# Mixer A: turning the attention probabilities with VectorE block transposes and placing copies instead of TensorE, with two query groups in flight

## The chip, the cores and the metric

The kernel runs on one core of one Trainium2 chip. The metric is the device time of one execution, in microseconds. The profiler gives the span of one execution beside it, with every instruction of TensorE (PE; weight loads: PEld), VectorE (DVE), ScalarE (ACT), GpSimd (POOL) and the DMA queue of SyncE (SP).

## The reference

The model is an encoder trunk of two layers on 256 tokens of 2048 features, in float32. Each layer is a token mixer and a gated MLP with a depthwise convolution, both behind an RMSNorm and with a residual add. The first layer uses mixer A, the second mixer B (three dilated head groups). The change is in mixer A: 16 query heads in 4 groups, each group with one key and one value head of 128 features; keys and queries are normalised per head and rotated.

```
def attend(q_blk):
    logits = jnp.einsum('bqkgd,bskd->bkgqs', q_blk, k).astype(jnp.float32) * scale
    p = jax.nn.softmax(logits, axis=-1).astype(v.dtype)
    return jnp.einsum('bkgqs,bskd->bqkgd', p, v)
```

Scores come out with queries on the partitions and keys along the free axis, which suits the softmax. The product with v sums over keys, so the probabilities have to be turned first: keys on the partitions. For one head that is a 256x256 transpose, held as two query halves m of 128 partitions by 256 keys.

## The kernel before

The tokens are split over 128 partitions and two halves m. Every float32 matmul is done as three products of rounded parts: an operand is split into a high part (ScalarE copy to fp32r) and a low part (VectorE subtraction), and TensorE adds high x high, high x low and low x high (L153 to L155 in `feed`, L307 to L309 in `mm3`). Weights come as 512 KB blocks through SP's queue (L145) into six raw tiles and are split by `split_raw` (L128 on ScalarE, L129 on VectorE) into a ring of three pairs wh, wl.

A projection (`project`) makes four calls of `feed` for one 512-wide output block. Each call issues two halves of 12 matmuls, and after each half it calls `step()`, so that a projection has eight steps. Work between projections is written as Python generators. `start` runs one to its first yield and puts it in the list `pending`; `step` advances the first of the list by one yield. If the list `wide` is not empty, `step` advances the first two instead. `drain` steps until the list is empty.

Mixer A first projects keys and values, then calls for the four query groups `start(attend(g, project(...)))`, then the output projection `out_proj`. So the attention of group g runs between the matmuls of projection g+1, and that of group 3 beside the first part of the output projection. `project2` in `out_proj` runs three quarters of two output blocks, drains, and then takes the last quarter, which reads the heads of group 3.

`attend(g)` begins with `qk_post`: ScalarE evacuates and squares, VectorE and GpSimd multiply with the rotary tables (L799, L804, L806), GpSimd raises to the power -0.5 (L390, its result rqk). Two steps later TensorE transposes the queries (`heads_T`, L703). Then come six stages, one step each: in stage k the scores, maxima and exps of head k (L846 to L860), the transposes of the probabilities of head k-1 (L868: four 128x128 TensorE transposes into a PSUM tile, then the split into pTh and pTl, L871), and the product with v for head k-2 with the split into its slot pair ah, al (L879 to L883). Nine steps in all, so a group's last stage falls on the first step of the next projection but one.

A second way of transposing exists already, `turned`, used for keys, for the residual and in mixer B: VectorE transposes all 32x32 blocks of a 128x512 half in one instruction each (L335), and `place_blocks` copies 16 sets of 32 partitions to where they belong. A string of four letters says which engine places which block: p is GpSimd, a ScalarE, v VectorE.

The order on each engine is not the order of the program. The framework has a planner that puts an instruction that is ready, by its own estimate of times, ahead of one that isn't, and otherwise goes by priority, which is program order. `split_raw` is given a priority 45 instructions earlier (AHEAD). Once planned, each engine runs its queue in order. The framework also sets the waits between engines by what is read and written of each tile, and gives a tile's place to its successor only when all its readers are done.

Slots: the pairs ah0 to ah23 and al0 to al23 hold the heads' outputs in mixer A (0 to 15) and mixer B (0 to 23), the activations in the MLP, and some probabilities in mixer B.

Of the kernel before, what the change touches and what calls it, by code (L numbers as in the profile page):

```python
# [7 lines left out]
F32 = mybir.dt.float32  # L8
# [25 lines left out]
def tile_encoder(ctx: ExitStack, tc: tile.TileContext, x, xT, w_a, w_ao, q_gain, k_gain, w_b, w_bo,  # L34
# [25 lines left out]
    def nm(s):  # L60
        uid[0] += 1
        return f"{s}_{uid[0]}"
# [353 lines left out]
    def ffn(l, hT, ss_in, g_next, last, side=None):  # L416
        with tc.tile_pool(name=nm("wpool"), bufs=1) as wp, tc.tile_pool(name=nm("fpool"), bufs=1) as fp:
# [101 lines left out]
            for hf, (p0, p1) in enumerate(HALVES):  # L519
# [197 lines left out]
    def mixer_a():  # L717
        with tc.tile_pool(name="apool", bufs=1) as ap:
# [110 lines left out]
            def attend(g, accs):  # L829
# [9 lines left out]
                prs, pTs, ots = {}, {}, {}  # L839
                for k in range(6):  # L840
                    yield
                    if k < 4:
                        i = k
                        s = ps_tile()
                        for m in range(2):
                            mm3(s[:, m * NT:(m + 1) * NT], qT, kT,  # L846
                                (slice(None), i, slice(m * P, (m + 1) * P)), (slice(None), g), True, True)
                        mx = small.tile([P, 2], F32, tag="mx", name=nm("mx"), bufs=3)
                        nc.vector.tensor_reduce(mx, s.rearrange("p (m c) -> p m c", m=2), axis=AX.X,
                                                op=ALU.max, negate=True)  # L850
                        nc.vector.tensor_tensor(mx, mx, rqv[:, :, i], ALU.mult)
                        pr = ap.tile([P, 2, NT], F32, tag="pr", name=nm("pr"), bufs=2)
                        l = small.tile([P, 2], F32, tag="l", name=nm("l"), bufs=3)
                        for m in range(2):
                            nc.scalar.activation(pr[:, m, :], s[:, m * NT:(m + 1) * NT], AF.Exp,
                                                 bias=mx[:, m:m + 1], scale=rq[:, 4 * m + i:4 * m + i + 1],
                                                 accum_out=l[:, m:m + 1])
                        nc.vector.reciprocal(l, l)
                        for m in range(2):
                            nc.vector.tensor_scalar(pr[:, m, :], pr[:, m, :], l[:, m:m + 1], None, op0=ALU.mult)  # L860
                        prs[i] = pr
                    if 1 <= k < 5:
                        i = k - 1
                        pr = prs.pop(i)
                        t = ps_tile()
                        for m in range(2):
                            for kt in range(2):
                                nc.tensor.transpose(t[:, kt * NT + m * P:kt * NT + (m + 1) * P],  # L868
                                                    pr[:, m, kt * P:(kt + 1) * P], ident)
                        pTs[i] = pair_tile(ap, [P, 2 * NT], "pT", 2)  # L870
                        split(pTs[i][0], pTs[i][1], t)  # L871
                    if k >= 2:
                        i = k - 2
                        pT = pTs.pop(i)
                        if i % 2 == 0:
                            ot = ps_tile()
# [261 lines left out]
```

## Time and profile before

| | us |
|---|---|
| median of 3 runs | 2264.49 (2264.11 to 2266.11) |
| profiled execution, its own time | 2266.43 |
| span of the profiled execution | 2264.6 |
| TensorE busy in the span | 2247.2 |
| VectorE busy | 1658.6 |
| ScalarE busy | 1511.0 |
| GpSimd busy | 257.7 |

The chain that ended last goes through TensorE for 80% of the span. Mixer A takes about the first 216 us; the probability transposes (L868) start between 93.7 and 198.5 us. A page row of an instruction group names line, engine, operation, the tiles, the shape and the count, then busy time and mean duration, then the idle time in front and what ended it. A row by source line or tile gives the least, median and longest duration in ns. A timeline row gives start, duration, engine, line and operation, with merged neighbours counted by x.

### The profile page before, as it was taken

What the parts mean: (1) busy time and instruction counts of PE and PEld (TensorE: products, weight loads), DVE (VectorE), ACT (ScalarE), POOL (GpSimd) and SP (SyncE); (2) the same over time, 40 slices, a digit from 0 to 9 for tenths busy, and PEclk for the clock granted to TensorE, in tenths of its full rate; (3) what the DMA queues carried; (4) which work ended last, traced back from release to release, by engine and by line L of the source; (5) the groups of instructions that cost most, each with busy time, mean ns of one, the idle gap of its engine ahead of it and who ended that gap; (6) DMA issues with size and microseconds to landing.
All of it is one profiled execution on the core that took longest, in us unless ns stands there. A gap on an engine that the chain in (4) does not pass through costs nothing.

```text
span 2264.6 us, 28910 instructions
## 1 busy us (share of the span) xinstructions
PE 2247.2 (99%) x10157; PEld 1859.7 (82%) x10157; DVE 1658.6 (73%) x2243; ACT 1511.0 (67%) x2344; POOL 257.7 (11%) x372
## 2 busy tenths in 40 slices
PE   9999999999999999999999999999999999999998
PEld 7788888888888888888888888888888888888886
DVE  6776687888878788856565556465888888688895
ACT  6665776777547777767755775565777754577763
POOL 2210112200001010121100100000101100001101
PEclk9999999999999999999999999999999999999999
DMA  8444557755665655666655564565656656556664
GB/s 299 156 149 150 197 196 224 223 188 190 209 205 187 201 189 188 208 218 203 192 172 178 177 193 160 183 195 187 196 192 194 204 186 212 188 191 193 218 202 135
DMA packets 126450, 437.43 MB, mean 193 GB/s; under 512 B 17264, under 2 KB 18032, under 8 KB 126304
## 3 DMA queue, kind: packets, MB, share of 16 engines
q1 hardware_dynamic: 119744, 425.64, 57.5%
q0 software_dynamic: 6128, 9.38, 1.6%
q8 instruction: 79, 1.29, 0.2%
q14 instruction: 67, 0.55, 0.1%
q10 hardware_dynamic: 432, 0.56, 0.1%
HBM read 429.20 MB, written 6.29 MB: 192 GB/s over the span
## 4 chain that ended last, share of the span: by engine, by line
PE 80%; DVE 1%; DMA 1%; ACT 1%; issue 1%; POOL 0%; POOLq 0%; DVEq 0%; ACTq 0%
PE acc L154 21%; PE acc L155 21%; PE acc L153 21%; PE acc L273 5%; PE acc L275 5%; PE acc L278 5%; DMA scr<-lnt 1%; PE ps L305 1%; DVE wl L129 1%; ACT tM L347 0%; PE ps L1016 0%; DMA raw<-in_w_down_dram 0%; ACT wh L128 0%; PE ps L308 0%; PE ps L309 0%
## 5 line engine op out<-in xcount | busy, mean ns | idle before, releaser
L129 DVE TENSOR_TENSOR wl<-raw,wh 128x1024 fp32r<-128x1024 f32 x828 | 1017.7, 1235 | 452.7 <-ACT wh L128 449.8
L128 ACT ACTIVATE wh<-raw 128x1024 fp32r<-128x1024 f32 x828 | 872.9, 1058 | 538.0 <-PE acc L155 325.8
L153 PE MATMUL acc<-wh,xh 128*128 128x512 f32 x2176 | 852.2, 392 | 0.2 <-ACT wh L164 0.2
L154 PE MATMUL acc<-wl,xh 128*128 128x512 f32 x2176 | 848.3, 390 | 3.1 <-DVE wl L129 2.9
L155 PE MATMUL acc<-wh,xh 128*128 128x512 f32 x2176 | 847.4, 389 | 0.0
L154 PEld LDWEIGHTS acc<-wl,xh 128*128 128x128 f32 x2176 | 408.7, 188 | 89.7 <-DVE wl L129 6.3
L155 PEld LDWEIGHTS acc<-wh,xh 128*128 128x128 f32 x2176 | 408.4, 188 | 84.9
L153 PEld LDWEIGHTS acc<-wh,xh 128*128 128x128 f32 x2176 | 408.9, 188 | 83.7 <-ACT wh L164 0.7
L345 POOL COPY u<-t 32x256 f32<-32x256 f32 x176 | 110.7, 629 | 1040.3 <-DVE t L455 1032.2
L273 PE MATMUL acc<-wh,ah 128*128 128x512 f32 x520 | 202.5, 389 | 1.3 <-DVE h L408 1.3
L275 PE MATMUL acc<-wh,al 128*128 128x512 f32 x520 | 202.3, 389 | 0.0
L154 PE MATMUL acc<-wl,ah 128*128 128x512 f32 x480 | 187.1, 390 | 1.0 <-DVE wl L129 1.0
L153 PE MATMUL acc<-wh,ah 128*128 128x512 f32 x480 | 187.3, 391 | 0.1
L155 PE MATMUL acc<-wh,al 128*128 128x512 f32 x480 | 186.6, 389 | 0.0
L347 ACT ACTIVATE u<-t 32x256 f32<-32x256 f32 x352 | 147.8, 420 | 13.8 <-DVE t L455 5.8
L278 PE MATMUL acc<-wl,ah 128*128 128x512 f32 x520 | 146.1, 389 | 0.0
L273 PEld LDWEIGHTS acc<-wh,ah 128*128 128x128 f32 x520 | 97.6, 188 | 22.2 <-DVE h L408 2.0
L278 PEld LDWEIGHTS acc<-wl,ah 128*128 128x128 f32 x520 | 97.6, 188 | 20.3
L275 PEld LDWEIGHTS acc<-wh,al 128*128 128x128 f32 x520 | 97.6, 188 | 20.2
L154 PEld LDWEIGHTS acc<-wl,ah 128*128 128x128 f32 x480 | 90.1, 188 | 20.1 <-DVE wl L129 1.8
L153 PEld LDWEIGHTS acc<-wh,ah 128*128 128x128 f32 x480 | 90.1, 188 | 19.0 <-DVE cu L628 0.6
L155 PEld LDWEIGHTS acc<-wh,al 128*128 128x128 f32 x480 | 90.1, 188 | 18.5
(180 smaller groups left out, 1666.4 us busy)
## 6 DMA issues: line engine op xcount, KB each, us to landing
raw<-in_w_up_dram SPq DMA_DIRECT2D x352, 512.0 KB, 4.3
raw<-in_w_down_dram SPq DMA_DIRECT2D x176, 512.0 KB, 4.8
raw<-in_w_b_dram SPq DMA_DIRECT2D x144, 512.0 KB, 4.3
raw<-in_w_bo_dram SPq DMA_DIRECT2D x48, 512.0 KB, 4.1
raw<-in_w_a_dram SPq DMA_DIRECT2D x40, 512.0 KB, 4.5
raw<-in_w_ao_dram SPq DMA_DIRECT2D x32, 512.0 KB, 3.8
raw<-in_w_a_dram SPq DMA_DIRECT2D x16, 256.0 KB, 6.5
h<-in_x_dram SPq DMA_DIRECT2D x4, 512.0 KB, 8.2
```

Of the source, the lines that this page charges most:

```text
L128: nc.scalar.activation(wh, r, AF.Copy)
L129: nc.vector.tensor_tensor(wl, r, wh.bitcast(F32), ALU.subtract)
L153: nc.tensor.matmul(accs[m], xh, wh[:, j, :], start=st, stop=False)
L154: nc.tensor.matmul(accs[m], xh, wl[:, j, :], start=False, stop=False)
L155: nc.tensor.matmul(accs[m], xl, wh[:, j, :], start=False, stop=sp)
L273: nc.tensor.matmul(acc[k], xh, wh[:, j, :], start=k in fresh, stop=False)
L275: nc.tensor.matmul(acc[k], xl, wh[:, j, :], start=False, stop=False)
L278: nc.tensor.matmul(acc[k], xh, wl[:, j, :], start=False, stop=last[k] == i and j == 1)
L305: nc.tensor.matmul(o, lh[ls], rh[rs], start=start, stop=stop)
L345: nc.gpsimd.tensor_copy(dst, src)
L347: nc.scalar.activation(dst, src, AF.Copy)
```

## The change

The probabilities of mixer A no longer go through TensorE. Per head, VectorE normalises them as before and then transposes all 32x32 blocks in one instruction. Per pair of heads, `place_blocks` with "papa" places 16 blocks, eight by GpSimd and eight by ScalarE. Then each head is split into pTh and pTl, from SBUF.

The stages become ten, one step each, with score of head 0 first and the value product of head 3 last. `wide` is set while mixer A's query groups run, so that two groups advance in each step; it is cleared when the first output block is done. The turned and the placed probabilities lie in four new tiles quad0 to quad3, which take the room of slots 16 to 23, two slots to a quad. These slots become views of the quads everywhere: in the MLP (`new_form`) and in mixer B (`slots`, and pr of its first and third group).

```diff
-    def new_slot(kt):
-        return (hpool.tile([P, NT], F32R, tag=f"ah{kt}", name=nm("ah")),
-                hpool.tile([P, NT], F32R, tag=f"al{kt}", name=nm("al")))
+    quads = {}
+
+    def new_quad(k):
+        return hpool.tile([P, 4, NT], F32, tag=f"quad{k}", name=nm("quad"))
+
+    def new_slot(kt, pool=hpool, dt=F32R):
+        if pool is not hpool or kt < 16:
+            return tuple(pool.tile([P, NT], dt, tag=f"a{c}{kt}", name=nm("a" + c)) for c in "hl")
+        k, i = divmod(kt - 16, 2)
+        if i == 0:
+            quads[k] = hpool.tile([P, 4, NT], dt, tag=f"quad{k}", name=nm("quad"))
+        return quads[k][:, 2 * i], quads[k][:, 2 * i + 1]
...
-                    return tuple(pool.tile([P, NT], F32R, tag=f"a{c}{k}", name=nm("a" + c)) for c in "hl")
+                    return new_slot(k, pool)
...
         def done(accs, n):
+            wide.clear()
             add_residual(accs, n)
...
-                        t = ps_tile()
-                        for m in range(2):
-                            for kt in range(2):
-                                nc.tensor.transpose(t[:, kt * NT + m * P:kt * NT + (m + 1) * P],
-                                                    pr[:, m, kt * P:(kt + 1) * P], ident)
-                        pTs[i] = pair_tile(ap, [P, 2 * NT], "pT", 2)
-                        split(pTs[i][0], pTs[i][1], t)
...
+                def score(i):
+                    if i % 2 == 0:
+                        parts["t", i // 2] = new_quad(i // 2).rearrange("p (m a) c -> p m (a c)", m=2)
...
+                def turn(i):
+                    pr, l = parts.pop(("pr", i)), parts.pop(("l", i))
+                    for m in range(2):
+                        nc.vector.tensor_scalar(pr[:, m, :], pr[:, m, :], l[:, m:m + 1], None, op0=ALU.mult)
+                    c = i % 2 * NT
+                    nc.vector.transpose(parts["t", i // 2][:, :, c:c + NT], pr)
+
+                def place(u):
+                    o = new_quad(2 + u)
+                    place_blocks(o.rearrange("p j (m t) -> p j m t", m=2), parts.pop(("t", u)), "papa")
+                    for i in range(2):
+                        parts[2 * u + i] = o[:, 2 * i:2 * i + 2].rearrange("p a t -> p (a t)")
+
+                def low(i):
+                    src = parts[i]
+                    parts[i] = pair_tile(ap, [P, 2 * NT], "pT", 2)
+                    split(*parts[i], src)
...
+                for fs in ((score, 0), (score, 1, turn, 0), (score, 2, turn, 1), (score, 3, place, 0, turn, 2),
+                           (turn, 3), (place, 1, low, 0), (low, 1, value, 0), (low, 2, value, 1),
+                           (low, 3, value, 2), (value, 3)):
+                    yield
+                    for f, a in zip(fs[::2], fs[1::2]):
+                        f(a)
+
+            wide.append(1)
             for g in range(4):
                 start(attend(g, project(w_a, g, hT, kgs)))
...
-                            pr = [hpool.tile([P, NT], F32, tag=f"a{c}{sl}", name=nm("pr")) for c in "hl"]
+                            pr = list(new_slot(sl, dt=F32))
...
-                            pt = hpool.tile([P, NT], F32, tag=f"ah{sl}", name=nm("pr"))
+                            pt = new_slot(sl, dt=F32)[0]
```

`score` and `value` hold the score and value code of before.

More of the change, by code (lines that the diff above doesn't have):

```diff
@@ new lines, in low, with value @@
+                def low(i):
+                    src = parts[i]
+                    parts[i] = pair_tile(ap, [P, 2 * NT], "pT", 2)
+                    split(*parts[i], src)
+                def value(i):
+                    pT, j = parts.pop(i), i % 2
+                    if j == 0:
+                        parts["o"] = ps_tile()
+                    ot = parts["o"]
+                    for kt in range(2):
+                        mm3(ot[:, j * NT:(j + 1) * NT], v, pT,
+                            (slice(None), kt, slice(g * P, (g + 1) * P)),
+                            (slice(None), slice(kt * NT, (kt + 1) * NT)), kt == 0, kt == 1)
+                    hi, lo = slots[4 * g + i]
+                    split(hi, lo, ot[:, j * NT:(j + 1) * NT])
```

54 lines of the change are left out of this document (17 added, 37 removed).

## The prediction

> **What bounds the kernel now.** I read the head of the page first: which engine fills the span.
>
> ```profile
> span 2264.6 us, 28910 instructions
> PE 2247.2 (99%) x10157; PEld 1859.7 (82%) x10157; DVE 1658.6 (73%) x2243; ACT 1511.0 (67%) x2344; POOL 257.7 (11%) x372
> ```
>
> TensorE is busy in 99% of the span, 17.4 us are left idle. So work taken off TensorE shortens the span, as long as nothing else makes TensorE wait. The change lies in mixer A alone, so the second view is the busy time by window, with windows cut from one first probability transpose of a query group to that of the next:
>
> ```profile
> core 0: us, PE busy (x) PEld busy (x) DVE busy (x) ACT busy (x) POOL busy (x), PEclk, DMA share, GB/s
> 93.69:124.45 30.76, 30.70 (x169) 26.07 (x169) 24.00 (x44) 19.84 (x39) 5.45 (x5) 1.00 0.42 137
> 124.45:155.21 30.76, 30.71 (x169) 26.07 (x169) 23.98 (x44) 19.83 (x39) 5.44 (x5) 1.00 0.43 138
> 155.21:185.97 30.76, 30.72 (x168) 26.06 (x169) 23.98 (x44) 19.83 (x39) 5.45 (x5) 1.00 0.42 139
> ```
>
> Each group takes 30.76 us, and TensorE is busy in 30.7 of it, at a granted clock of 1.00. VectorE has 6.8 us free per group, ScalarE 10.9, GpSimd 25. DMA has room (0.42). The third view is the waits of VectorE and ScalarE in these three periods (total us, times, longest):
>
> ```profile
> ACT wh L128 <- PE acc L155: 11.3, 9, 1.6
> ACT pr L855 <- DVE mx L851: 9.5, 12, 1.6
> DVE l L858 <- ACT pr L855: 8.0, 12, 1.3
> DVE rqk L831 <- POOL rqk L390: 4.3, 3, 1.4
> DVE ro L799 <- ACT stg L686: 3.5, 3, 1.2
> DVE mx L849 <- PE ps L309: 2.9, 6, 0.5
> DVE ro L806 <- POOL t L804: 1.2, 3, 0.4
> ```
>
> The five DVE rows sum to 19.9 us, 6.6 per group: all of VectorE's free time is waiting in its own queue, for exps, for scores, for the rotary part. This free time is what the change wants to use.
>
> **What is removed.** Sixteen heads lose their four TensorE transposes (L868). Matmuls are pipelined, so I price them by starts. These are rows of TensorE's timeline around the four heads of group 0: start, duration, instruction.
>
> ```profile
> 93.27 0.40 PE L154 MATMUL acc<-wl,xh 128*128 128x512 f32 x1
> 93.70 0.63 PE L868 MATMUL ps<-ident,pr 128*128 128x128 f32 x4
> ...
> 94.40 0.40 PE L153 MATMUL acc<-wh,xh 128*128 128x512 f32 x1
> 94.63 0.40 PE L154 MATMUL acc<-wl,xh 128*128 128x512 f32 x1
> ...
> 97.43 0.28 PE L309 MATMUL ps<-pTh,vl 128*128 128x256 f32 x1
> 97.55 0.65 PE L868 MATMUL ps<-ident,pr 128*128 128x128 f32 x4
> ...
> 98.16 0.28 PE L308 MATMUL ps<-pTl,vh 128*128 128x256 f32 x1
> ...
> 101.59 0.28 PE L308 MATMUL ps<-kTl,qTh 128*128 128x256 f32 x1
> 101.71 0.28 PE L309 MATMUL ps<-kTh,qTl 128*128 128x256 f32 x1
> 101.83 0.60 PE L868 MATMUL ps<-ident,pr 128*128 128x128 f32 x4
> ...
> 102.39 0.28 PE L308 MATMUL ps<-pTl,vh 128*128 128x256 f32 x1
> ...
> 105.50 0.39 PE L155 MATMUL acc<-wh,xh 128*128 128x512 f32 x1
> 105.90 0.63 PE L868 MATMUL ps<-ident,pr 128*128 128x128 f32 x4
> ...
> 106.49 0.29 PE L308 MATMUL ps<-pTl,vh 128*128 128x256 f32 x1
> ```
>
> Undisturbed, a 512-column matmul starts 0.23 us after the one before (94.40 to 94.63), a 256-column one 0.12 (101.59 to 101.71). Between the quoted neighbours lie two such spacings. Head 0: 94.40 - 93.27 - 2x0.23 = 0.67. Head 1: 98.16 - 97.43 - 2x0.12 = 0.49. Head 2: 102.39 - 101.71 - 2x0.12 = 0.44. Head 3: 106.49 - 105.50 - 0.23 - 0.12 = 0.64. Together 2.24 us per group; the periods are equal, so **4 x 2.24 = 9.0 us** over the four groups. The PSUM tile and its evacuation port fall away too; neither was waited for. The period that TensorE alone would allow is 30.76 - 2.24 = 28.5 us.
>
> **What is added on VectorE and ScalarE.** I quote the price of one block transpose and of the placing copies in mixer B and the output projection, and the splits from SBUF beside those from PSUM:
>
> ```profile
> L335 DVE STREAM_TRANSPOSE tT<-stg x24: 668/706/716, 1007.1 to 1336.0; 128x512 f32<-128x512 f32 x24
> 1009.99 2.71 POOL L345 COPY stg<-tT 32x256 f32<-32x256 f32 x4 [16.32 <-DVE tT L335]
> 1010.78 2.55 ACT L347 ACTIVATE stg<-tT 32x256 f32<-32x256 f32 x6
> L345 POOL COPY stg<-tT x16: 386/392/1425, 1010.0 to 1247.3; 32x256 f32<-32x256 f32 x16
> L129 DVE TENSOR_TENSOR wl<-raw,wh 128x1024 fp32r<-128x1024 f32 x8 | 9.7, 1218 | 0.0
> 220.46 1.36 DVE L129 TENSOR_TENSOR wl<-raw,wh 128x1024 fp32r<-128x1024 f32 x1 [0.67 <-ACT wh L128]
> L290 ACT ACTIVATE pTh<-ps 128x512 fp32r<-128x512 f32 x4 | 2.4, 601 | 1.0 <-PE ps L868 0.9
> L291 DVE TENSOR_TENSOR pTl<-ps,pTh 128x512 fp32r<-128x512 f32 x4 | 2.7, 683 | 0.0
> L291 DVE TENSOR_TENSOR al<-ps,ah 128x256 fp32r<-128x256 f32 x4 | 1.7, 414 | 0.0
> L290 ACT ACTIVATE ah<-ps 128x256 fp32r<-128x256 f32 x4 | 1.5, 382 | 0.1
> ```
>
> VectorE: one 128x512 transpose per head, 4 x 0.71 = 2.8 us per group. A split beside GpSimd copies took 1.36 us instead of 1.22; with two such meetings per placing and two placings, 4 x 0.14 = 0.6. ScalarE: with "papa" it places 8 of 16 blocks, at 2.55/6 = 0.425 each; two placings per group give 16 x 0.425 = 6.8 us. GpSimd: 8 blocks per placing, between 2.71 + 4x0.39 = 4.3 us (one stretched copy, as in the row) and 2 x 2.71 = 5.4 us (two), so 9 to 11 us per group on an engine with 25 free. The low split stays, 0.60 on ScalarE and 0.68 on VectorE, read from SBUF instead of PSUM; I leave it at that price.
>
> A full group (projections 2 and 3, where one group's score stages run beside the value stages of the one before) then holds: TensorE 28.5, VectorE 24.0 + 2.8 + 0.6 = 27.4, ScalarE 19.8 + 6.8 = 26.6, GpSimd 5.4 + 11 = 16. VectorE goes from 78% to 96%, ScalarE from 64% to 93%. In projection 1 the value stages are missing (4 x 0.68 and 4 x 0.41 = 4.4 less on VectorE, 23.0 of 28.5 - 24 x 0.12 = 25.6), and beside the output projection nothing is left of the rotary part; there is room there.
>
> The term that decides is how much VectorE still waits in a full group. Only 1.1 us is free. Lower end: no wait, as the second group always has something to issue; then 28.5. Upper end: all 6.6 us stay; then 34.0. I take the part that the other group cannot fill: the wait for the power on GpSimd (4.3/3 = 1.4) and for the rotary product (1.2/3 = 0.4), both at the group's head, both behind GpSimd, which now also places blocks. The exps' wait (2.7) and the scores' (1.0) lie where value stages of the other group can be put between. So VectorE needs 27.4 + 1.8 = 29.2, 0.7 over TensorE, in two full groups: **+1.4 us**. This is nearer to the lower end because the planner puts a ready instruction ahead of one that is not: the transposes of head 0 stand between two projection matmuls in the rows above.
>
> Trainium skill, "Perfetto Trace Analysis", section "Identifying the Most-Contended Engine": the engine with the highest occupancy is the one to relieve, and TensorE is to be judged by its weight loads rather than by its matmul time. Its weight loads here fill 26.07 of 30.76 us, 85%, so by that rule VectorE at 96% would be the bound in full groups, and the sum would follow VectorE's own queue, as in the second rival.
>
> **What is moved.** Ten stages instead of six per group: the last value stage comes four steps later, for group 3 in the drain ahead of the last quarter of the output projection. Its 8 blocks per engine are long placed by then; what may be late is the low split just before. The price is the one wait of TensorE for such a split:
>
> ```profile
> 89.00 0.39 PE L309 MATMUL ps<-kTh,qTl 128*128 128x256 f32 x1 [0.60 <-DVE qTl L291]
> ```
>
> Upper end: low split and value split both exposed, 0.60 + 0.68 + 0.38 + 0.41 = 2.1 us; lower end 0, since 12 projection matmuls can stand between. I take one such wait, **+0.6 us**. In projections 2 and 3 placing 1 queues on GpSimd behind the rotary products and perhaps ahead of the power; the score that needs the power follows four steps on, so nothing more is counted.
>
> Sharing four quad tiles instead of sixteen slot tiles makes a slot free only with its neighbour. In the MLP and mixer B both neighbours are read within one k-group and written again at least a projection later; 0, and if that cover were missing, one wait like the 0.60 above per quad. Clearing the wide mode happens with nothing pending: 0. No DMA is added, and none is moved past another.
>
> **Sum.** -9.0 + 1.4 + 0.6 = -7.0 us. The profiled execution took 2266.4 us (span 2264.6 and 1.8 around it), 1.9 over the median of 2264.5, within the spread of the runs. From the median: 2257.5; I round up to **2258**, since the waits can only be more than none.
>
> **Rivals.** First, full cover: VectorE and ScalarE always have something ready, 0 for both waits: -9.0, 2255.5. For it speaks the 10.9 us free on ScalarE; against it, that both engines then run above 92% in order.
>
> Second, the waits stay: 34.0 per full group, 3.2 more than now, twice: +6.5, against 4.5 won in the light groups 0 and 3, and 0.6 for the drain: +2.6, 2267. For it: the DVE rows above repeat in every group to 0.1 us, so they are part of the order. Against it: the order is made anew, with two groups to choose from.
>
> Third, on the other side: ScalarE waits in its queue for GpSimd's half. ScalarE's 8 blocks take 3.4 us, GpSimd's 4.3 to 5.4, so a low split queued right behind waits up to 2.0 us, the next raw split behind it, and VectorE's half of both. Twice per group that is 4.0 us; on top of 34.0 a full group takes 38.0, 7.2 more than now: 14.5 - 4.5 + 0.6 = +10.6, 2275. It decides from a full group of 35.0 us on: 2 x (35.0 - 30.76) - 4.5 + 0.6 = 4.6, 0.2% over. For it: "papa" gives GpSimd twice the blocks that any placing has now. Against it: the low split comes two steps, 24 matmuls of 0.23 or 5.5 us, after the placing.
>
> Trainium skill, "VectorE: DVE Perf Modes", sections "The three transpose paths" and "Rules for kernel authors": VectorE turns only 32x32 blocks, and a 128x128 transpose belongs on TensorE where PSUM is an acceptable destination. It was acceptable here, so the rule speaks for this third outcome; the trace so far shows 0.44 to 0.67 us a head for TensorE's way and more engine time for the other.
>
> Fourth, nothing moves: the planner displaces score and value matmuls so that the 9.0 us come back as waits for raw splits somewhere behind, 2264.
>
> **How the numbers follow.** Forecast (2256 to 2260) 0.42, full cover 0.15, waits stay or nothing moves 0.23 together, third rival 0.20. No change can be told within 0.2% or 4.5 us here. Faster: 0.42 + 0.15 = 0.57; same 0.23; slower 0.20. The range leaves out half of the third rival and the deep end of the first: 2254.5 to 2270. The forecast's own range is 2255.5 to 2260.
>
> **What would show it.** Right: no transposes of pr on TensorE; periods of projections 2 and 3 near 29.2 us, of projection 1 and the output projection 2.2 us shorter than now; VectorE above 92% in the full ones; the wait of l for pr much below 2.7 us a group; after the drain the timeline runs some 7 us earlier to the end. Wrong: TensorE waiting for wl (L129) or pT in full groups, each for over 0.5 us; ScalarE waiting for GpSimd's blocks; or the gain of mixer A lost again in the MLP, where I count nothing.

## The result, and the profile after

The changed kernel takes 2286.43 us, median of 5 runs (2283.84 to 2286.70), against 2265.63 for the kernel before (5 runs). The ratio is 1.0088, 95% interval 1.0074 to 1.0102: slower by 0.9%, where 2258 was forecast. The profiled execution has a span of 2284.6 us, 20.0 more than before.

The head of the page after, with two of its slice rows (busy tenths and granted clock in 40 slices):

```profile
span 2284.6 us, 28932 instructions
PE 2251.0 (99%) x10093; PEld 1860.5 (81%) x10093; DVE 1672.4 (73%) x2259; ACT 1536.7 (67%) x2408; POOL 293.8 (13%) x436
...
PE   9988999999999999999999999999999999999998
...
PEclk9989999999999999999999999999999999999999
```

TensorE has 64 instructions fewer, as it should (16 heads x 4), and yet it is busy 3.8 us longer. The low digits that concern the change stand in the third and fourth slice, 114 to 228 us: mixer A. The first residual add of its output projection starts at 216.2 us before and at 237.4 after, 21.2 later; from there to the end the changed kernel is 1.2 us quicker. So the whole loss lies in mixer A. I use this start as a second measure below ("mixer A ends").

The windows of 10 us through that stretch (TensorE busy, weight loads, VectorE, ScalarE, GpSimd, each with its count, then the granted clock, DMA share, GB/s), of after:

```profile
core 0: us, PE busy (x) PEld busy (x) DVE busy (x) ACT busy (x) POOL busy (x), PEclk, DMA share, GB/s
100.00:110.00 10.00, 9.05 (x40) 6.85 (x38) 8.07 (x14) 9.84 (x21) 6.62 (x13) 1.00 0.33 105
110.00:120.00 10.00, 5.02 (x22) 3.98 (x23) 5.82 (x8) 5.84 (x11) 6.19 (x8) 0.84 0.17 55
120.00:130.00 10.00, 10.00 (x47) 8.43 (x46) 6.71 (x12) 4.22 (x8) 0.00 (x0) 0.82 0.45 137
...
150.00:160.00 10.00, 7.45 (x25) 5.62 (x24) 5.82 (x9) 5.73 (x10) 4.80 (x7) 0.54 0.28 84
...
180.00:190.00 10.00, 6.58 (x28) 5.03 (x28) 8.99 (x9) 9.80 (x21) 8.44 (x12) 0.92 0.15 52
...
86.00:237.00 151.00, 132.97 (x632) 109.62 (x631) 110.69 (x188) 104.42 (x214) 52.44 (x79) 0.92 0.39 125
```

and the same four groups of before in one window:

```profile
86.00:216.00 130.00, 129.22 (x697) 109.29 (x696) 96.87 (x172) 78.79 (x150) 16.34 (x15) 1.00 0.44 144
```

Two things are new. TensorE stands still for 18.0 of 151 us, against 0.8 of 130. And its granted clock, 1.00 throughout before, has a mean of 0.92, with 0.54 in one window. Over the stretch no other engine is full: VectorE is busy 110.69 of 151 us (73%), ScalarE 69%. Only in windows in which a stall begins is one of them full (ScalarE 9.84 of 10 from 100 us and 9.80 from 180). What TensorE waits for is in the view of waits, 70 to 250 us, of after (total us, times, longest):

```profile
DVE rqk L841 <- POOL rqk L399: 12.8, 4, 4.2
...
PE ps L308 <- DVE pTl L291: 7.1, 3, 3.6
PE ps L713 <- DVE ro L816: 6.9, 3, 3.1
...
DVE l L868 <- ACT pr L865: 6.3, 6, 1.3
...
PE ps L307 <- ACT pTh L290: 2.1, 1, 2.1
```

TensorE waits for the low part of the turned probabilities (pTl) and for the rotated queries (ro), and VectorE itself waits 12.8 us for the power on GpSimd. How these hang together is seen in the timeline at the head of projection 2 (start, duration, instruction, and the idle time before it), of after:

```profile
105.73 3.82 POOL L814 TENSOR_TENSOR t<-stg,st_q 128x256 f32<-128x256 f32 x4 [3.09 <-ACT stg L696]
109.50 5.31 POOL L354 COPY quad<-quad 32x256 f32<-32x256 f32 x8
114.89 1.63 POOL L399 TENSOR_TENSOR rqk<-ms,nhalf 128x8 f32<-128x8 f32 x1
...
110.89 0.37 DVE L398 TENSOR_SCALAR ms<-ssq 128x8 f32<-128x8 f32 x1
111.17 1.21 DVE L129 TENSOR_TENSOR wl<-raw,wh 128x1024 fp32r<-128x1024 f32 x1
116.56 0.17 DVE L841 TENSOR_SCALAR rqk<-rqk 128x8 f32<-128x8 f32 x1 [4.18 <-POOL rqk L399]
116.64 1.28 DVE L291 TENSOR_TENSOR pTl<-quad,pTh 128x512 fp32r<-128x512 f32 x2
...
108.30 3.40 ACT L356 ACTIVATE quad<-quad 32x256 f32<-32x256 f32 x8
111.72 1.15 ACT L290 ACTIVATE pTh<-quad 128x512 fp32r<-128x512 f32 x2
...
113.35 0.39 PE L155 MATMUL acc<-wh,xh 128*128 128x512 f32 x1
117.38 0.58 PE L308 MATMUL ps<-pTl,vh 128*128 128x256 f32 x1 [3.64 <-DVE pTl L291]
...
119.04 0.63 PE L154 MATMUL acc<-wl,xh 128*128 128x512 f32 x1
119.47 0.63 PE L155 MATMUL acc<-wh,xh 128*128 128x512 f32 x1
```

Read it from the bottom up. TensorE's value product starts late because pTl is late. Its other operand part, pTh, is ready at 112.87. But in VectorE's queue a small instruction stands ahead of the low split: the scaling of rqk (L841, 0.17 us), which needs the power. The power's input ms is there at 111.26, but GpSimd has eight placing copies in front of it, and begins it at 114.89. So a third engine's copies hold up two splits and two raw splits that have nothing to do with it. After the stall, 512-column matmuls start 0.43 us apart instead of the 0.23 of the kernel before.

### The profile page after: what moved, and what is told of

The parts are those of the page before. It is cut to its first block, busy times and chain, and to the rows that moved or that the text cites. A ratio compares the mean times of both kernels' runs of the same rounds, so it can differ in the third digit from the quotient of the medians.

```text
span 2284.6 us, 28932 instructions
## 1 busy us (share of the span) xinstructions
PE 2251.0 (99%) x10093; PEld 1860.5 (81%) x10093; DVE 1672.4 (73%) x2259; ACT 1536.7 (67%) x2408; POOL 293.8 (13%) x436
## 4 chain that ended last, share of the span: by engine, by line
PE 80%; DVE 1%; DMA 1%; ACT 1%; issue 0%; POOL 0%; POOLq 0%; DVEq 0%; ACTq 0%
PE acc L154 21%; PE acc L153 21%; PE acc L155 21%; PE acc L273 5%; PE acc L275 5%; PE acc L278 5%; DMA scr<-lnt 1%; PE ps L305 1%; ACT tM L356 0%; DVE wl L129 0%; PE ps L1040 0%; PE ps L308 0%; ACT wh L128 0%; PE ps L309 0%; PE ps L307 0%
## 5 line engine op out<-in xcount | busy, mean ns | idle before, releaser
L154 PE MATMUL acc<-wl,ah 128*128 128x512 f32 x368 | 144.5, 393 | 1.0 <-DVE wl L129 1.0
L153 PE MATMUL acc<-wh,ah 128*128 128x512 f32 x368 | 143.9, 392 | 0.4 <-ACT wh L128 0.4
L155 PE MATMUL acc<-wh,al 128*128 128x512 f32 x368 | 143.5, 391 | 0.0
L273 PE MATMUL acc<-wh,ah 128*128 128x512 f32 x364 | 141.8, 390 | 1.1 <-DVE h L417 1.1
L275 PE MATMUL acc<-wh,al 128*128 128x512 f32 x364 | 141.6, 389 | 0.0
L278 PE MATMUL acc<-wl,ah 128*128 128x512 f32 x364 | 103.3, 389 | 0.0
L154 PEld LDWEIGHTS acc<-wl,ah 128*128 128x128 f32 x368 | 69.7, 189 | 15.8 <-DVE wl L129 1.8
L463 ACT ACTIVATE s<-acc,rstd 128x512 f32<-128x512 f32 x88 | 59.7, 679 | 33.2 <-PE acc L155 33.2
L153 PEld LDWEIGHTS acc<-wh,ah 128*128 128x128 f32 x368 | 69.3, 189 | 15.2 <-ACT wh L128 0.8
L155 PEld LDWEIGHTS acc<-wh,al 128*128 128x128 f32 x368 | 69.6, 189 | 14.3
L273 PEld LDWEIGHTS acc<-wh,ah 128*128 128x128 f32 x364 | 68.3, 188 | 15.9 <-DVE h L417 1.7
L278 PEld LDWEIGHTS acc<-wl,ah 128*128 128x128 f32 x364 | 68.3, 188 | 14.2
```

Of the source, the lines that this page charges most:

```text
L153: nc.tensor.matmul(accs[m], xh, wh[:, j, :], start=st, stop=False)
L154: nc.tensor.matmul(accs[m], xh, wl[:, j, :], start=False, stop=False)
L155: nc.tensor.matmul(accs[m], xl, wh[:, j, :], start=False, stop=sp)
L273: nc.tensor.matmul(acc[k], xh, wh[:, j, :], start=k in fresh, stop=False)
L275: nc.tensor.matmul(acc[k], xl, wh[:, j, :], start=False, stop=False)
L278: nc.tensor.matmul(acc[k], xh, wl[:, j, :], start=False, stop=last[k] == i and j == 1)
```

## The experiments

Three theories were set against each other. **A**, the queue: the placing delays the power, the scaling waits at the head of VectorE's queue, and with it all that is behind. **B**, the load: the placing copies are simply too much work for ScalarE and GpSimd, wherever they stand. **C**, the interleave: running two groups in each step, in ten stages, disturbs the projection at its head, whoever turns the probabilities. Ratios are against the kernel before, measured on the same chip; beside the experiments its medians were 2265.2 to 2266.3 us, so a difference between two experiments carries about 1 us from the chip alone.

### Which part of the change costs: the interleave, the turning, the placing

First, everything of the change but the turning: ten stages, two groups per step and quads stay, and TensorE turns the probabilities as before.

```diff
...
 def low(i):
-    src = parts[i]
+    pr = parts.pop(("pr", i)); t = ps_tile()
+    for m in range(2):
+        for kt in range(2):
+            nc.tensor.transpose(t[:, ...], pr[:, m, kt * P:(kt + 1) * P], ident)
     parts[i] = pair_tile(ap, [P, 2 * NT], "pT", 2)
-    split(*parts[i], src)
+    split(*parts[i], t)
...
```

> The changed kernel with the probabilities turned by TensorE again, in the stage of the low split, and no placing; the ten stages, the two groups side by side and the quads stay. Theory A (the placing copies are the cause): GpSimd and ScalarE are as free as in the kernel before, no wait for rqk over 2 us, 2262 to 2268 us, that is, the kernel before within 0.2%. Theory B (ScalarE's load): the same, 2262 to 2268. Theory C (the interleave): over 2275 us, with TensorE waiting at the head of each projection for ro and pTl as in the changed kernel.

Measured: 2278.21 us, ratio 1.0060 (1.0043 to 1.0077); mixer A ends at 224.9. The waits of this kernel that matter:

```profile
PE ps L308 <- DVE pTl L291: 8.2, 3, 2.7
DVE rqk L841 <- POOL rqk L399: 6.1, 4, 1.5
```

The interleave alone costs 8.7 us by the end of mixer A in the profiled execution (224.9 - 216.2). That was the fastest of four (2273.2 us; the others 2276.3 to 2280.7, at a lower mean granted clock, 0.996 to 0.997 against 0.998), so by the medians the cost is 12.9. Three stalls of 2.7 us stand at the heads of projections 2 and 3 and of the output projection (they end at 112, 145 and 180 us), although nothing is placed and the wait for the power is short (1.5 each).

Next, the change without its placing copies: VectorE turns the blocks, and the low split reads them where they are. The copies are what is left out, so the output isn't the attention's.

```diff
...
 def place(u):
-    o = new_quad(2 + u)
-    place_blocks(o.rearrange(...), parts.pop(("t", u)), "papa")
+    o = parts.pop(("q", u))
+    parts.pop(("t", u))
...
```

> The changed kernel without the placing copies: the low split takes the turned 32x32 blocks as they lie, so the output isn't the attention's; the 128 copies of 32x256 on GpSimd and ScalarE are left out and nothing else. Theory A and B (the copies, on GpSimd or ScalarE, make the loss): the 9.0 us of the transposes show, 2255 to 2262 us. Theory C (the interleave of one group's tail with the next one's head on VectorE costs by itself, as the run with TensorE transposes in the same stages, 2278 us, suggests): 2278 less 9, so 2266 to 2272 us.

Measured: 2265.43 us, ratio 1.0003 (0.9990 to 1.0016): the time of the kernel before, and in neither of the two expected ranges. Mixer A ends at 216.7. A window of 10 us ahead of a stall and that of its four groups, then TensorE's two largest waits:

```profile
100.00:110.00 10.00, 9.47 (x46) 7.65 (x44) 9.96 (x15) 8.45 (x15) 4.20 (x4) 1.00 0.33 105
...
86.00:216.00 130.00, 121.61 (x631) 102.63 (x630) 109.14 (x187) 76.54 (x150) 18.66 (x15) 1.00 0.46 145
```

```profile
PE acc L154 <- DVE wl L129: 5.6, 5, 1.6
PE ps L307 <- DVE al L291: 3.2, 3, 1.3
```

This orders the whole difference. By the end of mixer A, in the profiled executions: 216.2 before; 224.9 with the interleave (+8.7); 216.7 when VectorE turns instead of TensorE (-8.2, near the 9.0 of the forecast's first term; by the medians +12.9 and -12.8); 237.4 with the copies (+20.7). TensorE's 9.0 us are won and lost again: TensorE stands still 8.4 of 130 us here. The stalls are about as long in sum as those of the interleave with TensorE's own transposes, but they aren't the same ones: TensorE now waits for low splits of the weights (wl) and of the heads' outputs (al), behind a VectorE that was full for 10 us (9.96 here, 9.92 and 9.93 ahead of the next two heads). That is the bound of the forecast's second rival, in bursts. The copies then cost 20.7 us, though they run on ScalarE and GpSimd alone.

### Theory A: the scaling behind the power

One word of the changed kernel is edited, so that the scaling runs on GpSimd, right behind the power it needs. Nothing of the order on TensorE, ScalarE or SyncE changes.

```diff
 ro, rq = qk_post(accs, "q")
-nc.vector.tensor_scalar(rq, rq, SCALE, None, op0=ALU.mult)
+nc.gpsimd.tensor_scalar(rq, rq, SCALE, None, op0=ALU.mult)
```

> The changed kernel with one instruction per query group moved: the multiplication of rqk by the scale goes from VectorE to GpSimd, right behind the power. TensorE's, ScalarE's and SP's queues keep their order word for word, VectorE's loses four instructions. Theory A (VectorE's queue stands still behind GpSimd, which places blocks ahead of the power; that stall costs TensorE its time and then its clock): VectorE's waits for rqk (12.8 us in the changed kernel) fall below 3 us, TensorE's waits for pTl and pTh (9.2 us) below 2 us, the granted clock falls less often, and the time is 2266 to 2275 us. Theory B (ScalarE, at 93% of a full group, is the bound): VectorE then waits for ScalarE instead, TensorE's idle time stays above 14 us in mixer A, and the time stays within 4 us of 2286. Theory C (two groups side by side bunch the head of one with the tail of the other, whatever the transposes do): no less than 2280 us.

Measured: 2274.72 us, ratio 1.0042 (1.0027 to 1.0057); mixer A ends at 224.3. TensorE's waits that remain:

```profile
PE ps L713 <- DVE ro L816: 6.9, 3, 3.1
PE ps L307 <- ACT pTh L290: 2.1, 1, 2.1
```

The wait of VectorE for rqk is gone, and with it TensorE's three waits for pTl. 11.7 us of 20.8 go with one instruction of 0.17 us, more than half of the loss.

The control makes the same edit in the kernel before:

> The kernel before with the scaling of rqk on GpSimd, a control for the run that moved it in the changed kernel. VectorE loses its 5.8 us of waits for rqk, TensorE had nothing to wait for: if the gain there came from the stall behind the placing, the time here stays at 2265 us, within 3. If it came from taking work off VectorE as such, it falls by some 6.

Measured: 2264.82 us, ratio 0.9995 (0.9985 to 1.0004). In the kernel before the edit is worth nothing, so what it saves after is the stall and not the instruction.

The converse: in the kernel before, make the power late and change nothing else. Eight GpSimd instructions stand between the rotary product and the power of each query and key group; they write the exponent -0.5 that it reads.

```diff
+nh = hpool.tile([P, NT], F32, tag="ah23", name=nm("nh"))
+for i in range(8):
+    a = slice(32 * (i % 4), 32 * (i % 4) + 32)
+    nc.gpsimd.tensor_scalar(nh[a], ro[a, i // 4, :NT], 0.0, -0.5, op0=ALU.mult, op1=ALU.add)
...
-rsqrt_mean(r, ssq, P)
+rsqrt_mean(r, ssq, P, nh[:, :8])
```

> The kernel before with eight GpSimd operations of 32x256 elements put between the rotary product and the power of each query and key head group (they make the operand -0.5 of the power out of ro, so they can neither start earlier nor end later). Nothing else changes: transposes on TensorE, one group at a time. It holds the suspected cause alone: the power comes some 4 us later. Theory A: VectorE waits for rqk 4 us more per group, TensorE loses at least half of that each time and then clock; 2272 to 2285 us. Theories B and C: VectorE has 6.6 us free per group and ScalarE 10.9, so under 2267 us.

Measured: 2284.79 us, ratio 1.0090 (1.0067 to 1.0112), with mixer A's end at 231.9 in the profiled execution, which was the fastest of four (2280.6). Its waits:

```profile
DVE rqk L835 <- POOL rqk L390: 16.7, 4, 4.9
...
PE ps L309 <- DVE qTl L291: 9.8, 4, 3.6
```

A late power alone makes the tuned kernel as slow as the change does, by the same path: VectorE waits at rqk, and here the low part of the queries (qTl), behind it, is late for the scores. It is enough by itself for such a loss, and some 12 us of the change's go with it: theory A is shown from both sides for that part.

### Theory B: the load of the placing

The copies of one engine at a time, added to the kernel without placing; what they write isn't read, so again the output isn't the attention's.

```diff
 def place(u):
     o = parts.pop(("q", u))
-    parts.pop(("t", u))
+    place_blocks(new_quad(2 + u).rearrange(...), parts.pop(("t", u)), "papa", only)
...
```

Here `only` leaves the blocks of the other engine out. GpSimd's 64 copies:

> The changed kernel with ScalarE's half of the placing left out; GpSimd's 64 copies write into the quads, and nobody reads them: the low split takes the turned blocks as they lie, so the output isn't the attention's. Against the run without any copies (2265.4 us) it adds GpSimd's queue alone. If the power behind the copies is the main cost: 2274 to 2282 us, with the waits of VectorE for rqk back at 12 us. If ScalarE's copies are: 2265 to 2269.

ScalarE's 64 copies:

> The same with GpSimd's half left out and ScalarE's 64 copies kept, unread. If ScalarE's burst at the head of a projection is the main cost: 2274 to 2282 us, with TensorE waiting for wh, wl or pTh; if GpSimd's queue is: 2265 to 2270 us. If both count, the two increments over 2265.4 add up to about the 21 us that all copies cost.

Measured: GpSimd's half 2276.24 us, ratio 1.0042 (1.0027 to 1.0057), mixer A's end at 226.3; ScalarE's half 2272.14, ratio 1.0027 (1.0016 to 1.0038), at 222.1. One row of the waits of each, first of GpSimd's half:

```profile
DVE rqk L843 <- POOL rqk L401: 10.2, 4, 2.9
```

and of ScalarE's half:

```profile
PE ps L715 <- DVE ro L818: 5.3, 3, 1.8
```

Against the kernel without placing the halves cost 10.8 and 6.7 us, 17.5 together, of the 21.0 of both. GpSimd's copies act mainly through the power: VectorE's wait for it is 10.2 us against 6.1 without copies, and TensorE's wait for al, whose split stands behind the scaling, 5.1 against 3.2. ScalarE's act through the rotary part: TensorE waits 5.3 us for ro, and not at all without copies. By the order of ScalarE's queue they hold up the evacuations that ro is made from. In both the granted clock falls (a mean of 0.96 and 0.98 from 86 to 225 us), which it doesn't without copies (1.00).

All 16 blocks on ScalarE, which takes theory A's cause away and doubles ScalarE's load:

```diff
-place_blocks(o.rearrange(...), parts.pop(("t", u)), "papa")
+place_blocks(o.rearrange(...), parts.pop(("t", u)), "aaaa")
```

> The changed kernel with all 16 blocks of a placing on ScalarE and none on GpSimd. ScalarE gets 16 x 0.425 = 6.8 us more per group, 33.4 in a full one, where TensorE has 28.5 to do; GpSimd goes back to its load before the change. Theory A: the wait of VectorE for rqk falls below 2 us in all; what is left is ScalarE's own queue, 33.4 - 30.8 = 2.6 us over the old period in two full groups, so 2268 to 2280, below the changed kernel. Theory B: ScalarE was the bound already, so its further 27 us show nearly whole: over 2295 us.

Measured: 2294.27 us, ratio 1.0131 (1.0115 to 1.0146), mixer A's end at 243.0.

```profile
PE acc L153 <- ACT wh L128: 12.6, 4, 4.0
...
DVE rqk L841 <- POOL rqk L399: 6.3, 4, 1.8
```

The wait for the power is back at 6.3 us, the level of the kernel before (5.8) though not below 2 as expected, and a new one is larger: TensorE waits 12.6 us for the high part of the weights, which ScalarE makes behind up to 11 copies in a row (4.7 us). So 2294.27 is far over A's 2268 to 2280 and just under B's 2295: here ScalarE's load decides.

### Moving the placing, and halving it

Two attempts to get the burst away from the head of the projection. One more step before the queries are turned, and the first two low splits a step earlier, so that the number of stages stays (a group may take no more than 13 steps, as the output projection then reads its heads):

```diff
 yield
 yield
+yield
 for _ in heads_T(qT, ro):
...
-           (turn, 3), (place, 1, low, 0), (low, 1, value, 0), (low, 2, value, 1),
+           (turn, 3, low, 0), (place, 1, low, 1, value, 0), (low, 2, value, 1),
```

> The changed kernel with the query transposes one step later and the tail closed up by one step (low split of head 0 joins the last turn; the second placing comes with the value stage of head 0), thirteen steps as before. In GpSimd's queue the rotary products and the power now stand ahead of the second placing. All work of the changed kernel is done. Theory A (the order at the head of a projection: power behind the placing, query transposes too early): VectorE's waits for rqk fall from 12.8 to some 6 us, as in the kernel before, TensorE's waits for ro (6.9) and pTl (7.1) to under 2 us together, and the time is 2262 to 2272 us. Theory B (ScalarE, 93% of a full group): the waits turn up at wh and pTh instead, over 2275 us.

Measured: 2282.18 us, ratio 1.0073 (1.0058 to 1.0088). VectorE's wait for the power is down to 6.1 us, as theory A asked, but the time is 10 us over A's range and only 4.3 below the change: TensorE now waits for wh (5.2 us) and still for ro (3.5). Taking the late power away is thus not enough where the move makes other things late. The same with the scaling on GpSimd:

> Both mends at once: the query transposes one step later and the scaling of rqk on GpSimd. Theory A: VectorE has no wait for rqk left; 1 to 4 us below the run with the later query transposes alone, 2259 to 2270 us, at best the 9.0 us of the transposes less some 3 of waits, that is, 6 us below the kernel before. Theory B: no difference from that run.

Measured: 2278.12 us, ratio 1.0058 (1.0042 to 1.0075): no better than the scaling's edit alone (2274.72; the two intervals overlap), as the burst now falls on other waits (ScalarE waits 9.2 us for GpSimd's blocks, VectorE 14.5 us for exps). And that with three of four blocks on GpSimd ("ppap"):

> Both mends, and GpSimd places 12 of 16 blocks, ScalarE 4: 8 x 0.425 = 3.4 us per group less on ScalarE, 3 to 5 more on GpSimd. Theory B: ScalarE's load is what is left, so 3 to 8 us faster than both mends with half and half. Theory A (GpSimd's queue): the low split waits for the blocks, up to 7.5 us after the turn, and it is 2 to 8 us slower.

Measured: 2297.78 us, ratio 1.0148 (1.0130 to 1.0165). One of its waits:

```profile
ACT pTh L290 <- POOL quad L354: 18.1, 5, 4.4
```

The forecast's third rival, ScalarE waiting for GpSimd's blocks, is a large wait only here: 18.1 us. In the change itself it doesn't appear.

Last, half the change without the interleave: six stages and one group per step as before, heads 0 and 1 of a group turned by VectorE and placed once, heads 2 and 3 by TensorE.

```diff
-for fs in ((score, 0), ..., (score, 3, place, 0, turn, 2),
-           (turn, 3), (place, 1, low, 0), (low, 1, value, 0), (low, 2, value, 1),
-           (low, 3, value, 2), (value, 3)):
+for fs in ((score, 0), ..., (score, 3, place, 0, turn, 2),
+           (turn, 3, value, 2, low, 0, value, 0), (value, 3, low, 1, value, 1)):
...
-wide.append(1)
```

> Half of the change, away from the head of the projections: heads 0 and 1 of each group are turned by VectorE and placed with papa in the stage of score 3, heads 2 and 3 by TensorE as before; six stages and one group at a time, as in the kernel before. Saved: 0.67 + 0.49 us per group, 4.6 in all. Theory A with C (what hurts is work queued at the head of a projection, beside the rotary part and the power): no wait for rqk beyond the 1.5 us per group of the kernel before, and 2259 to 2265 us. Theory B (placing on ScalarE hurts wherever it stands): 2270 us or more.

Measured: 2276.21 us, ratio 1.0046 (1.0031 to 1.0061), mixer A's end at 225.1. Two windows of it:

```profile
100.00:110.00 10.00, 9.38 (x48) 6.90 (x47) 7.37 (x13) 9.86 (x21) 6.89 (x10) 1.00 0.18 52
...
120.00:130.00 10.00, 10.00 (x54) 8.62 (x53) 7.72 (x16) 5.96 (x13) 0.00 (x0) 1.00 0.61 199
```

Neither the head of the projection nor the interleave is there, the wait for the power is 6.1 us, the clock stays at 1.00, and it is still slower. So A and C aren't all of it. Load is what B would say, but the edit has a second effect that no run separates from it: the low split of a head and the value product that reads it now stand in the same step, and of TensorE's waits 4.8 us in six times are for pTl and 2.7 in eight for the normalised probabilities. Where placing runs (100 to 110) ScalarE is full, and TensorE looks 94% busy with weight loads in only 6.90 us, against 8.62 where nothing is placed. Trainium skill, "Perfetto Trace Analysis", section "Identifying the Most-Contended Engine": TensorE's headroom is read from its weight loads, since pipelined matmuls make its busy time a poor measure. These two rows agree: 1.7 us of loads per 10 are missing, and only 0.6 of busy time.

### The granted clock

To see whether the half clock after a stall costs time by itself, 72 matmuls without use were put ahead of the stalls of the changed kernel (16 ahead of a first value product, 8 ahead of turning the queries).

```diff
+def fill(n):
+    d = ps_tile()
+    for _ in range(n):
+        nc.tensor.matmul(d, v[0][:, 0, :P], v[0][:, 0, :], start=True, stop=True)
...
```

> The changed kernel with idle work for TensorE at the two places where it stood still: 8 matmuls of 512 columns ahead of the query transposes of groups 1 to 3, 16 ahead of the first value product of groups 0 to 2, into a PSUM tile that nobody reads: 72 matmuls, 72 x 0.227 = 16.3 us of TensorE. If TensorE's clock falls because it stands still, and that costs 12 us of the loss: the granted clock stays at 0.95 or more in the 10 us windows of mixer A, the filling takes the place of idle time, and the time falls to 2274 to 2282 us. If the clock has nothing to do with standing still, or costs little: 2286 to 2302 us.

Measured: 2302.11 us, ratio 1.0167 (1.0150 to 1.0184). They ran before the stalls rather than in them; 72 x 0.23 = 16 us were added, about the whole increase over the change (15.7), and TensorE's waits for pTl grew from 7.1 to 12.8 us. Nothing follows for the clock.

The second attempt measures it in the kernel before: one small matmul per group waits for a chain of 1, 2, 4 and 6 GpSimd powers, so that TensorE alone stands still, with no work added to VectorE or ScalarE. The scaling writes a tile of its own, so as not to wait for the chain.

```diff
+z = rq
+for _ in range((1, 2, 4, 6)[g]):
+    y, z = z, small.tile([P, 8], F32, tag="z", name=nm("z"), bufs=2)
+    nc.gpsimd.tensor_tensor(z, y, nhalf, ALU.pow)
+nc.tensor.matmul(ps_tile()[:, :8], ident, z, start=True, stop=True)
...
```

> The kernel before, in which one small matmul per query group waits for a chain of 1, 2, 4 and 6 powers on GpSimd (1.6 us each), behind the power of rqk, so that nothing but TensorE waits for it: four stalls of growing length with no load on VectorE or ScalarE. If TensorE's clock falls after standing still: the granted clock is 1.00 after the shortest and between 0.5 and 0.9 in the 10 us after the longest stalls, and the time grows by more than the idle time, 2275 to 2295 us. If not: clock 1.00 throughout, and the growth is the idle time.

Measured: 2314.23 us, ratio 1.0210 (1.0194 to 1.0225), mixer A's end at 257.0, 40.8 later. The waits, then windows of 2 us around the second stall, then TensorE's timeline there:

```profile
PE ps L835 <- POOL z L834: 31.7, 4, 12.5
```

```profile
120.00:122.00 2.00, 0.79 (x4) 0.33 (x2) 1.15 (x3) 0.81 (x1) 1.09 (x1) 1.00 0.77 229
122.00:124.00 2.00, 0.00 (x0) 0.00 (x0) 1.32 (x2) 0.00 (x0) 1.92 (x2) 0.78 0.59 217
124.00:126.00 2.00, 0.00 (x0) 0.00 (x0) 0.00 (x0) 0.00 (x0) 1.89 (x2) 0.50 0.46 154
126.00:128.00 2.00, 1.98 (x6) 1.69 (x7) 0.00 (x0) 0.00 (x0) 0.00 (x0) 0.50 0.37 139
128.00:130.00 2.00, 2.00 (x8) 1.51 (x7) 0.00 (x0) 0.16 (x1) 0.00 (x0) 0.52 0.00 0
130.00:132.00 2.00, 2.00 (x14) 1.77 (x13) 1.07 (x1) 1.87 (x3) 0.00 (x0) 1.00 0.00 0
```

```profile
120.40 0.39 PE L154 MATMUL acc<-wl,xh 128*128 128x512 f32 x1
126.02 0.60 PE L835 MATMUL ps<-z,ident 128*128 128x8 f32 x2 [5.23 <-POOL z L834]
...
127.05 0.63 PE L153 MATMUL acc<-wh,xh 128*128 128x512 f32 x1
127.47 0.63 PE L154 MATMUL acc<-wl,xh 128*128 128x512 f32 x1
...
131.10 0.39 PE L155 MATMUL acc<-wh,xh 128*128 128x512 f32 x1
131.33 0.39 PE L153 MATMUL acc<-wh,xh 128*128 128x512 f32 x1
```

TensorE stood still for 31.7 us, and mixer A ends 40.8 us later: 9.1 us more, 2.3 per stall. In the stall shown the clock falls to 0.50 some 2.3 us in and stays there for 4 us after it, with matmuls 0.42 us apart; then it is 1.00, with 0.23. Worked out from windows like these for all four stalls (4.7, 5.2, 9.3 and 12.5 us long), the clock falls 2.3 to 4.3 us in, and TensorE then works at half clock for 5.5, 3.9, 3.4 and 5.5 us. Half of that sum is 9.1 us, the whole excess. Trainium skill, "TensorE: Matmul & The Clock Gate", section "HAM oscillation — how this bites in real kernels": gaps of TensorE of over about 3.4 us bring it back to half clock. The traces agree only in part. The four stalls here and the 3.64 us stall of the changed kernel have the half clock behind them. But in the run with TensorE's own transposes one of the three stalls of 2.7 us, the one that ends at 145 us, is too (0.50 from 146 to 148), and the two others aren't; and in the changed kernel a stall of 2.1 us that ends at 222 us is (a mean of 0.83 from 220 to 230). A single long gap isn't needed either: in the changed kernel the clock also fell at 150.9 us, after four microseconds of little work with no wait above 1.9 us in it (TensorE busy 1.78 us from 146 to 150). So the length of the stall alone doesn't tell, in these traces, whether the clock falls.

No version that does all the work was faster than the kernel before.

## Why the prediction was wrong

**The removed transposes: right.** The first term was -9.0 us. Inside the same interleave, giving them up moved mixer A's end by -8.2 (224.9 to 216.7), and the median by -12.8; that this is more than 9.0 comes with the stalls and the clock of the run it is compared with, so it isn't a closer measure of the term.

**The step that failed** is this one: "In projections 2 and 3 placing 1 queues on GpSimd behind the rotary products and perhaps ahead of the power; the score that needs the power follows four steps on, so nothing more is counted." The order on GpSimd is as it says. But the score isn't the first to need the power. The scaling of rqk on VectorE is, and it stands in an in-order queue ahead of the low splits that the next value product wants. I asked who needs the result, and not what is queued behind the first instruction that waits for it. The row was on the table: VectorE's wait for rqk, 4.3 us in three times (5.8 in four), rose to 12.8 in four. Moving the scaling took back 11.7 us; delaying the power in the kernel before cost 19.5.

**VectorE's remaining waits, +1.4: wrong in the sum, right in part.** The waits for exps, which were said to be filled by the other group, did fall (8.0 us in 12 times in three groups, to 6.3 in 6 times in four). The argument for the low end, that "the planner puts a ready instruction ahead of one that is not", doesn't hold across engines: the scaling was put ahead of a split that was ready 3.8 us earlier. That the planner's estimate of GpSimd's queue was off is argued from this, not shown.

**The loads: a mean over a group hid the burst.** VectorE at 96% and ScalarE at 93% were derived for full groups; the group stretched, and both stayed near 70%. What counted was ScalarE full for 10 us at each head of a projection, where eight copies stand ahead of evacuations, splits and raw splits. The copies were costed by their engine time and compared with an engine's free time per group; on the chip they made mixer A end 20.7 us later.

**The interleave: not costed at all.** It was treated as the way in which waits get filled. It costs 8.7 us by itself in the profiled execution (12.9 by the medians), in three stalls of 2.7 us at the heads of the blocks that follow.

**The clock: not in the sum.** It cost 10.3 us by the account below, and 2.3 us a stall where it was measured alone.

**What was costed at nothing or little and was so:** the quads in the MLP and mixer B (the rest of the kernel is 1.2 us quicker), and the drain, in which TensorE doesn't wait.

**The rivals.** The third had the sign and named ScalarE's queue, but its mechanism, ScalarE waiting for GpSimd's blocks, isn't in the waits of the change. It appears when the scaling is moved (2.5 us), when the placing is moved (7.8 and 9.2) and, large, when GpSimd gets more blocks. Its price of 2275 was 11 us short. The second, 2267, was built from VectorE's queue as bound. VectorE is 73% busy in the change and at most 91% in any window of 10 us from 70 to 240 us, so there order and not occupancy set the time; in the kernel without placing VectorE is the bound in bursts, and TensorE waits 8.8 us for it. The rule that a 128x128 transpose belongs on TensorE (Trainium skill, "VectorE: DVE Perf Modes", "Rules for kernel authors") had the better forecast: even half the heads, without the interleave, cost 11 us.

An account of the 21.2 us: TensorE's still time rose by 17.2 (0.8 to 18.0), the transposes gave 9.0 back, and the clock took 10.3 (TensorE was at work for 20.6 us of the four stretches at half clock that windows of 1 and 2 us show from 116.7 to 226 us; half of that is lost). That is 18.5; 2.7 us stay unexplained. **Open:** how the rest beside theory A's 12 us splits between the interleave and the load, since the parts aren't additive (10.8 + 6.7 against 21.0); how the 11 us of the half change divide between load and its own order; why the interleave makes its three stalls; and what decides whether a stall of 2 to 3 us is followed by the half clock.

## What to carry to other kernels

Before work is moved onto an engine "with room", list what each other engine has queued behind its first wait for that engine: an in-order queue turns a tiny instruction with a late input into a stall of everything behind it. Read room in windows as short as the burst that you add, not per stage, and ask what stands just before the stage's head. Where one engine bounds the kernel at 99%, a stall can cost more than its length: count the half clock that may follow it.

## What the runs showed of the hardware

In a kernel that keeps TensorE 99% busy, the clock fell to 0.50 from 2.3 to 4.3 us into four long stalls and stayed there for 3 to 6 us after them (2.3 us lost per stall); stalls of 2.1 to 2.7 us were followed by it in some cases and not in others. GpSimd's 32x256 copies took 0.39 us at the median and up to 1.46, a mean of 0.58 over the 64 of the change. The rotary multiplication on VectorE (L799 before, L809 after) took up to 3.60 us instead of 1.76 at most; the longest one ran beside GpSimd's rotary products and its first placing copies, and without any copies all four took 1.76 to 1.78. Which of the two engines holds the other up wasn't tried apart. TensorE's weight loads showed the small gaps of the half change (6.90 us in 10 against 8.62), which its busy time hid.
